# A retention layer's prompt states, computed from split keys and values as single-rate matrix products

## The chip, the cores and the metric

The kernel runs on one core of a Trainium2 chip. The metric is the device time of one execution in microseconds (us); lower is better. A core has five engines with queues of their own: TensorE (PE, matrix products; its weight loads are listed as PEld), VectorE (DVE), ScalarE (ACT), GpSimd (POOL) and SyncE (SP), which here issues the DMA transfers. SBUF is the memory on the core, PSUM the memory that TensorE writes its products to.

## The reference, cut to what matters

One layer of a hybrid decoder: a feed-forward half step, a mixer, another feed-forward half step, each with a layer norm. The mixer runs a retention branch (8 heads, keys and values 256 wide) beside an HGRN2 branch (16 heads of 128). It handles 16 meta tokens and 256 prompt tokens, and 8 sample sequences of one token each. For each retention head the prompt leaves a state, the sum over the prompt's tokens of key (outer) value, each key scaled by the head's decay up to the last token:

```
def retention_chunk(S, q, k, v):
    ...
    k_dec = k * jnp.exp(lg[:, None] * (C - 1.0 - idx))[:, :, None].astype(k.dtype)
    S_new = jnp.exp(lg * C)[:, None, None].astype(S.dtype) * S + jnp.einsum('bhjd,bhjv->bhdv', k_dec, v)
    return S_new.astype(S.dtype), o
```

These states (`state_ret_prompt`, 8 heads of 256 x 256) are one of the six outputs. All numbers are float32.

## The kernel before

Activations lie with features on the partitions and the 280 tokens (272 prompt, 8 samples) along the free axis. Every large weight is read in units of eight 128x128 blocks (512 KB): SyncE loads a unit into `raw` (three buffers), ScalarE rounds it to the single-rate type float32r (`whi`, line 145), and VectorE takes the difference (`wlo`, line 147). Activations are split in the same way. A dense product is then three single-rate products per block: high x high, high x low, low x high (lines 169 to 171). `whi` and `wlo` have three buffers each.

The order of TensorE's instructions is that in which the program emits them. The other engines' and SyncE's orders are laid out by a scheduler at build time, in which the weight units have high priority; each engine then executes its queue in order, and each instruction waits for its operands.

In the mixer the input projection is the dense stream, head by head: for head u the groups f, q_h, i_h, q_r, k_r, v_r, then the gates of head u - 1. Beside it run two "threads", Python generators: `mix_hg` (HGRN2) and `mix_ret` (retention). After each k step of the dense stream (in a group of two outputs that is six products), `pump` counts down each thread's wait; when it is zero, the thread emits its next piece. `yield 12` thus means that the thread's next piece stands 12 steps later in TensorE's order.

`mix_ret` for one head, with the names used below:

- For each half c of the 256 features: values are transposed on TensorE in three blocks of tokens (128, 128, and the last 24: 16 prompt tokens and 8 samples) into a PSUM bank `pt` and copied by ScalarE into `vtr` and `vt2` (lines 711, 712). Keys are transposed likewise, and VectorE multiplies them by the decay `dec` into `ktr` and `kt2` (line 718). The decay of the 8 samples' rows is zero. PSUM banks of the tag `mx` go round in four, for both threads.
- Scores: products of keys and queries (`psc`), multiplied by the table `dtab`.
- States: for each half, three full-precision products of keys and values into `psr` (line 743), copied to `sro` and written out (lines 746, 747).
- Samples, in two parts e of four samples: `vbr` holds the sample's value on all partitions (read back by a DMA). For each half, `smr` (three buffers of 512 KB) receives four samples' states by DMA (line 761), ScalarE scales it by the decay (line 762), VectorE adds key times value (line 765), and it is written out (line 768). After `yield 12` TensorE multiplies it with the queries (`pqr`, line 774).
- Outputs of the prompt (`por`), norm (`pvr`) and the rest.

In `mix_hg`, the product `po` of line 681 reads `osh`, which ScalarE copies in line 674 from `pq`.

Of the kernel before, what the change touches and what calls it, by code (L numbers as in the profile page):

```python
# [10 lines left out]
F32 = mybir.dt.float32  # L11
F32R = mybir.dt.float32r
U8 = mybir.dt.uint8
AF = mybir.ActivationFunctionType
ALU = mybir.AluOpType
# [3 lines left out]
P = 128  # L19
# [78 lines left out]
def trunk(ctx: ExitStack, tc: tile.TileContext, A, O):  # L98
    nc = tc.nc
# [12 lines left out]
    def mx_bank(name):  # L112
        return ps_m.tile([P, 512], F32, tag="mx", name=name)
# [12 lines left out]
    dec = cst.tile([P, 3, HR], F32, tag="dec", name="dec")  # L126
# [48 lines left out]
    def split(hi, lo, x):  # L175
        nc.scalar.copy(hi, x)  # L176
        nc.vector.tensor_tensor(out=lo, in0=x, in1=hi.bitcast(F32), op=ALU.subtract)  # L177
# [6 lines left out]
    def mul(out, a, b):  # L184
        nc.vector.tensor_tensor(out=out, in0=a, in1=b, op=ALU.mult)
# [4 lines left out]
    def sub(out, a, b):  # L190
        nc.vector.tensor_tensor(out=out, in0=a, in1=b, op=ALU.subtract)  # L191
# [195 lines left out]
    with tc.tile_pool(name="yp", bufs=1) as yp:  # L387
        yh, yl = [None] * KC, [None] * KC
        with tc.tile_pool(name="mp", bufs=1) as mp:
# [7 lines left out]
            def tmp(name, shape=(P, T), bufs=1, dt=F32, tag=None):  # L397
                if name in rows:
                    rows[name] = rows[name][1:] + rows[name][:1]
                    return rp.tile(list(shape), dt, tag=rows[name][-1], name=name)  # L400
                return mp.tile(list(shape), dt, tag=tag or name, name=name, bufs=bufs)
# [24 lines left out]

            km = tmp("km", (P, P))
            vm = tmp("vm", (P, 2, 2, P))
            kt2 = tmp("kt2", (P, 2, P))
            vt2 = tmp("vt2", (P, 2, P))  # L430
            scr2 = tmp("scr2", (P, NMETA))
            for z in (km, vm, kt2, vt2, scr2):
                nc.gpsimd.memset(z, 0.0)
            threads = []

            def pump(_=None):
# [87 lines left out]
            BLOCKS = ((0, P), (P, P), (2 * P, T - 2 * P))  # L524

            def rows_out(src, width, tag):

                scr = drp.tile([NS, width], F32, tag=tag + "d", name=tag + "d")
                nc.sync.dma_start(scr, src)
                return scr  # L530
# [170 lines left out]

            def mix_ret(u, q, k, v):
                vt = tmp("vtr", (P, 2, 2, P))
                kt = tmp("ktr", (P, 2, 2, P))
                dt = tmp("dtab", (P, NSC))
                nc.sync.dma_start(dt, A["dtab"][u])
                for c in range(2):
                    pt = mx_bank("pt")
                    for b, (t0, n) in enumerate(BLOCKS):
                        nc.tensor.transpose(pt[:n, b * P : (b + 1) * P], v[:, c, t0 : t0 + n], ident)  # L710
                    nc.scalar.copy(vt[:, :, c, :], pt[:, : 2 * P].rearrange("p (b f) -> p b f", b=2))
                    nc.scalar.copy(vt2[: BLOCKS[2][1], c, :], pt[: BLOCKS[2][1], 2 * P : 3 * P])
                    yield 1
                    pt = mx_bank("pt")
                    for b, (t0, n) in enumerate(BLOCKS):
                        nc.tensor.transpose(pt[:n, b * P : (b + 1) * P], k[:, c, t0 : t0 + n], ident)
                    for b, (t0, n) in enumerate(BLOCKS):
                        nc.vector.tensor_scalar(
                            out=(kt[:, b, c, :] if b < 2 else kt2[:n, c, :]), in0=pt[:n, b * P : (b + 1) * P],
                            scalar1=dec[:n, b, u : u + 1], scalar2=None, op0=ALU.mult)  # L720
                    yield 2
                nc.vector.tensor_copy(qdr[:, :, 0 : NS * 32 : 33], q[:, :, SEQ:])
                vts = [vt[:, 0], vt[:, 1], vt2]
                kts = [kt[:, 0], kt[:, 1], kt2]
                vrow = rows_out(vt2.rearrange("p c f -> p (c f)")[16:24, :], 256, "vr")

                psc = mx_bank("psc")
                for b, (col, l0, n, nk) in enumerate(SCORES):
                    for c in range(2):
                        nc.tensor.matmul(  # L730
                            psc[:nk, col : col + n], k[:, c, b * P : b * P + nk], q[:, c, l0 : l0 + n],
                            start=c == 0, stop=c == 1)
                scr = dt
                c2 = SCORES[2][0]
                mul(scr[:, :c2], psc[:, :c2], dt[:, :c2])
                mul(scr2[:NB2], psc[:NB2, c2:NSC], dt[:NB2, c2:])
                scrs = [scr[:, SCORES[0][0] : SCORES[1][0]], scr[:, SCORES[1][0] : c2], scr2]
                yield 2

                for c in range(2):  # L740
                    pst = mx_bank("psr")
                    for b in range(3):
                        nc.tensor.matmul(
                            pst[:, :256], kts[b][:, c, :], vts[b].rearrange("p c f -> p (c f)"), start=b == 0, stop=b == 2)
                    so = tmp("sro", (P, 256))
                    nc.scalar.copy(so, pst[:, :256])
                    nc.sync.dma_start(O["srp"][u, c], so)
                    yield 2

                centre(vt.rearrange("p b c f -> p b (c f)"))  # L750
                centre(vt2.rearrange("p c f -> p (c f)").unsqueeze(1))

                os = tmp("osr", (P, 256))
                for e in range(2):
                    vb = tmp("vbr", (P, 4, 256))
                    nc.sync.dma_start(vb, vrow[4 * e : 4 * e + 4, :].partition_broadcast(P))
                    sms = []
                    for c in range(2):
                        sm = tmp("smr", (P, 4, 256), bufs=3)
                        sms.append(sm)  # L760
                        nc.sync.dma_start(sm, A["sr"][u, c, :, 4 * e : 4 * e + 4, :])
                        nc.scalar.mul(sm, sm, GAMMA[u])
                        for j in range(4):
                            t = LP + 4 * e + j
                            nc.vector.scalar_tensor_tensor(  # L765
                                out=sm[:, j, :], in0=vb[:, j, :], scalar=k[:, c, t : t + 1], in1=sm[:, j, :],
                                op0=ALU.mult, op1=ALU.add)
                        nc.sync.dma_start(O["srs"][u, c, :, 4 * e : 4 * e + 4, :], sm)
                    yield 12
                    pq = mx_bank("pqr")  # L770
                    for c in range(2):
                        for j in range(4):
                            b = 4 * e + j
                            nc.tensor.matmul(
                                pq[32 * j : 32 * j + 32, :256], qdr[:, c, 32 * b : 32 * b + 32], sms[c][:, j, :],
                                start=c == 0, stop=c == 1, tile_position=(0, 32 * j))
                    if e == 0:
                        nc.scalar.copy(os, pq[:, :256])
                    else:
                        add(os, os, pq[:, :256])  # L780
                centre(os.unsqueeze(1))
                yield 7

                on = tmp("on_r", (P, 2, TL), bufs=2)
                on_r[u] = on
                for c in range(2):
                    po = mx_bank("por")
                    for b, (col, l0, n, nk) in enumerate(SCORES):
                        nc.tensor.matmul(po[:, l0 : l0 + n], vts[b][:, c, :], scrs[b], start=b == 0, stop=b == 2)
                    nc.tensor.matmul(po[:, SEQ:TL], os[:, c * P : (c + 1) * P], sel, start=True, stop=True)  # L790
                    nc.scalar.copy(on[:, c, :], po[:, :TL])
                    yield 1
                sqs = tmp("sqr", (P, TL)), tmp("sq2", (P, TL))
                for c in range(2):
                    nc.scalar.activation(sqs[c], on[:, c, :], AF.Square)
                add(sqs[0], sqs[0], sqs[1])
                hilo = tmp("rhi", (P, TL), dt=F32R), tmp("rlo", (P, TL), dt=F32R)
                split(*hilo, sqs[0])
                yield 7
                pv = mx_bank("pvr")  # L800
                sums(pv[:, :TL], hilo)
                r = rsqrt(lambda name: tmp(name, (P, TL)), pv[:, :TL], 1.0 / 256, eps_h)
                for c in range(2):
                    mul(on[:, c, :], on[:, c, :], r)
                done_r.add(u)
# [131 lines left out]
```

## Time and profile before

| | |
|---|---|
| median of 3 runs | 2847.35 us (2843.78 to 2848.24) |
| the profiled execution | 2841.64 us |
| its span, first to last instruction | 2839.6 us |
| granted TensorE clock | 0.997 |
| busy share: TensorE, VectorE, ScalarE | 98%, 60%, 46% |
| HBM traffic | 188 GB/s over the span |

Rows of the profile name a source line of the kernel, the engine, the operation, output<-inputs by the program's names, the tile (partitions x elements) and the count. In a list of groups follow the busy time in us and the mean ns of one instruction, then the engine's idle time before them and what ended it. In a list in order of time the first number is the start in us, the second the length of the merged rows, and a bracket gives the idle time before and its releaser. Names that differ only in digits are merged, so `vt2` is shown as vt, `kt2` as kt, and the three groups of `pt` banks as pt. Products overlap in TensorE's pipeline, so the distance between two starts tells what a product costs in a stream, not the length of its row. "SPq" is SyncE's queue of DMA issues.

### The profile page before, as it was taken

The numbers are of one execution on the slowest core, as the hardware profiler recorded it, in microseconds if no ns is written. First come the engines' busy times: TensorE is split into PE (matmuls) and PEld (weight loads), VectorE is DVE, ScalarE is ACT, GpSimd is POOL, SyncE is SP. The second block draws the span as 40 slices with busy tenths as digits, with TensorE's granted clock in tenths as the row PEclk, the third lists the DMA queues.
The fourth block names the chain that finished last, engine by engine and source line by source line (L and its number), as shares of the span: only waits on it lengthen the run. The fifth ranks groups of instructions, "written<-read, shape, count | busy, mean of one in ns | idle before, by whom it ended". The sixth has DMA issues, their size and how long they took to land. (4 is left out here: it accounts for less than half of the span.)

```text
span 2839.6 us, 54221 instructions
## 1 busy us (share of the span) xinstructions
PE 2796.7 (98%) x22626; PEld 2760.7 (97%) x22626; DVE 1712.0 (60%) x2754; ACT 1317.9 (46%) x1921; POOL 4.5 (0%) x43
## 2 busy tenths in 40 slices
PE   8999999999999999999999999999999999999997
PEld 8999999999999999999999999999999999999997
DVE  5444444455578767666766676765884444445555
ACT  4443444433354564545454555545554444444333
POOL 0000000000000000000000000000000000000000
PEclk9999999999999999999999999999999999999998
DMA  6455555445555665756565657565555555555553
GB/s 214 171 171 171 170 170 171 170 168 171 170 193 189 221 241 178 244 177 241 178 240 184 239 180 245 179 217 171 179 178 182 180 184 180 183 180 180 181 182 128
DMA packets 155718, 536.26 MB, mean 189 GB/s; under 512 B 18064, under 2 KB 27856, under 8 KB 155472
## 3 DMA queue, kind: packets, MB, share of 16 engines
q1 hardware_dynamic: 155472, 532.80, 55.4%
q8 instruction: 177, 2.90, 0.4%
q14 instruction: 69, 0.57, 0.1%
HBM read 502.12 MB, written 30.61 MB: 188 GB/s over the span
## 5 line engine op out<-in xcount | busy, mean ns | idle before, releaser
L147 DVE TENSOR_TENSOR wlo<-raw,whi 128x1024 fp32r<-128x1024 f32 x868 | 1063.1, 1225 | 899.4 <-ACT whi L145 895.6
L145 ACT CAST whi<-raw 128x1024 fp32r<-128x1024 f32 x868 | 909.0, 1047 | 1160.3 <-PE up L170 481.8
L169 PE MATMUL up<-xh,whi 128*128 128x280 f32 (+1 forms) x2688 | 773.2, 288 | 8.6 <-ACT xh L176 8.6
L170 PE MATMUL up<-xl,whi 128*128 128x280 f32 (+1 forms) x2688 | 774.5, 288 | 1.3 <-DVE xl L177 1.2
L171 PE MATMUL up<-xh,wlo 128*128 128x280 f32 (+1 forms) x2688 | 773.6, 288 | 0.0
L169 PEld LDWEIGHTS up<-xh,whi 128*128 128x128 f32 x2688 | 506.8, 189 | 8.6 <-ACT xh L176 8.6
L170 PEld LDWEIGHTS up<-xl,whi 128*128 128x128 f32 x2688 | 506.5, 188 | 2.1 <-DVE xl L177 2.1
L171 PEld LDWEIGHTS up<-xh,wlo 128*128 128x128 f32 x2688 | 506.8, 189 | 0.0
L169 PE MATMUL dn<-hh,whi 128*128 128x280 f32 (+1 forms) x1376 | 397.1, 289 | 0.0
L170 PE MATMUL dn<-hl,whi 128*128 128x280 f32 (+1 forms) x1376 | 395.8, 288 | 0.0
L171 PE MATMUL dn<-hh,wlo 128*128 128x280 f32 (+1 forms) x1376 | 395.7, 288 | 0.0
L170 PEld LDWEIGHTS dn<-hl,whi 128*128 128x128 f32 x1376 | 259.0, 188 | 0.1
L169 PEld LDWEIGHTS dn<-hh,whi 128*128 128x128 f32 x1376 | 258.9, 188 | 0.1
L171 PEld LDWEIGHTS dn<-hh,wlo 128*128 128x128 f32 x1376 | 258.6, 188 | 0.0
L765 DVE SCALAR_TENSOR_TENSOR smr<-vbr,k_r,smr 128x256 f32<-128x256 f32 x128 | 54.1, 480 | 55.2 <-DMA vbr<-vrd 33.6
L169 PE MATMUL pj_g_r<-xh,whi 128*128 128x264 f32 x256 | 82.9, 324 | 0.0
L170 PE MATMUL pj_i_h<-xl,whi 128*128 128x280 f32 x256 | 74.9, 293 | 2.6 <-DVE xl L324 2.6
L169 PE MATMUL pj_v_r<-xh,whi 128*128 128x280 f32 x256 | 76.6, 299 | 0.0
L169 PE MATMUL pj_i_h<-xh,whi 128*128 128x280 f32 x256 | 75.0, 293 | 0.7 <-ACT xh L323 0.7
L169 PE MATMUL pj_k_r<-xh,whi 128*128 128x280 f32 x256 | 75.2, 294 | 0.0
L171 PE MATMUL pj_v_r<-xh,wlo 128*128 128x280 f32 x256 | 74.6, 291 | 0.0
L170 PE MATMUL pj_v_r<-xl,whi 128*128 128x280 f32 x256 | 74.6, 291 | 0.0
(324 smaller groups left out, 5178.0 us busy)
## 6 DMA issues: line engine op xcount, KB each, us to landing
raw<-in_w_up SPq DMA_DIRECT2D x344, 512.0 KB, 3.5
raw<-in_w_in SPq DMA_DIRECT2D x320, 512.0 KB, 3.6
raw<-in_w_dn SPq DMA_DIRECT2D x172, 512.0 KB, 3.4
smr<-in_sr SPq DMA_DIRECT2D x32, 512.0 KB, 7.1
out_srs<-smr SPq DMA_DIRECT2D x32, 512.0 KB, 3.4
raw<-in_w_out SPq DMA_DIRECT2D x32, 512.0 KB, 3.4
smh<-in_sg SPq DMA_DIRECT2D x16, 512.0 KB, 4.3
out_sgs<-smh SPq DMA_DIRECT2D x16, 512.0 KB, 4.3
```

Of the source, the lines that this page charges most:

```text
L145: nc.scalar.copy(hi, raw)
L147: nc.vector.tensor_tensor(out=lo, in0=raw, in1=hi.bitcast(F32), op=ALU.subtract)
L169: nc.tensor.matmul(o, wh, h, start=k == 0, stop=False)
L170: nc.tensor.matmul(o, wh, l, start=False, stop=False)
L171: nc.tensor.matmul(o, wl, h, start=False, stop=k == nk - 1)
L765: nc.vector.scalar_tensor_tensor(out=sm[:, j, :], in0=vb[:, j, :], scalar=k[:, c, t : t + 1], in1=sm[:, j, :], op0=ALU.mult, op1=ALU.add)
```

## The change

For the retention states alone, keys and values are split into a high part (rounded to float32r) and a low part (the difference). For each of the two full token blocks and each half there are three single-rate products (high x high, high x low, low x high). The last block has only 24 rows, so its three products are stacked in one: the key tile `ks2` holds high, high, low at rows 0, 32 and 64, and the value tile `vs2` holds high, low, high; the rest of both is zero. A half's state is then seven single-rate products in place of three full-precision ones. The high parts of the keys come from ScalarE (`activation` with the decay as scale), the low parts from VectorE. The split tiles `ks` and `vs` use two of the three buffers of the tag `smr`, and the wait ahead of the sample products is 14 steps in place of 12. `vtr` and `vt2` stay, as the prompt's outputs still read them; `ktr` and `kt2` go.

```
-            kt2 = tmp("kt2", (P, 2, P))
...
+            ks2 = tmp("ks2", (P, 2, P), dt=F32R)
+            vs2 = tmp("vs2", (P, 2, P), dt=F32R)
+            for z in (km, vm, vt2, scr2):
                 nc.gpsimd.memset(z, 0.0)
+            for z in (ks2, vs2):
+                nc.scalar.copy(z.rearrange("p c f -> p (c f)"), vm.rearrange("p h b f -> p (h b f)")[:, : 2 * P])
...
             def mix_ret(u, q, k, v):
                 vt = tmp("vtr", (P, 2, 2, P))
-                kt = tmp("ktr", (P, 2, 2, P))
+                ks, vs = (tmp(n, (P, 2, 2, 2 * P), dt=F32R, bufs=3, tag="smr") for n in ("ks", "vs"))
+                NB = BLOCKS[2][1]
+                third = [slice(32 * i, 32 * i + NB) for i in range(3)]
...
                     nc.scalar.copy(vt[:, :, c, :], pt[:, : 2 * P].rearrange("p (b f) -> p b f", b=2))
-                    nc.scalar.copy(vt2[: BLOCKS[2][1], c, :], pt[: BLOCKS[2][1], 2 * P : 3 * P])
+                    nc.scalar.copy(vt2[:NB, c, :], pt[:NB, 2 * P : 3 * P])
+                    f = slice(c * P, (c + 1) * P)
+                    split(vs[:, 0, :, f], vs[:, 1, :, f], vt[:, :, c, :])
+                    nc.scalar.copy(vs2[third[0], c, :], vt2[:NB, c, :])
+                    nc.scalar.copy(vs2[third[2], c, :], vt2[:NB, c, :])
+                    sub(vs2[third[1], c, :], vt2[:NB, c, :], vs2[third[0], c, :].bitcast(F32))
                     yield 1
...
                     for b, (t0, n) in enumerate(BLOCKS):
-                        nc.vector.tensor_scalar(
-                            out=(kt[:, b, c, :] if b < 2 else kt2[:n, c, :]), in0=pt[:n, b * P : (b + 1) * P],
-                            scalar1=dec[:n, b, u : u + 1], scalar2=None, op0=ALU.mult)
+                        x, g = pt[:n, b * P : (b + 1) * P], dec[:n, b, u : u + 1]
+                        his = [ks[:, 0, b, f]] if b < 2 else [ks2[third[0], c, :], ks2[third[1], c, :]]
+                        for hi in his:
+                            nc.scalar.activation(hi, x, AF.Copy, scale=g)
+                        nc.vector.scalar_tensor_tensor(
+                            out=(ks[:, 1, b, f] if b < 2 else ks2[third[2], c, :]), in0=x, scalar=g,
+                            in1=his[0].bitcast(F32), op0=ALU.mult, op1=ALU.subtract)
...
                 for c in range(2):
                     pst = mx_bank("psr")
-                    for b in range(3):
-                        nc.tensor.matmul(
-                            pst[:, :256], kts[b][:, c, :], vts[b].rearrange("p c f -> p (c f)"), start=b == 0, stop=b == 2)
+                    f = slice(c * P, (c + 1) * P)
+                    pairs = [(ks[:, i, b, f], vs[:, j, b, :]) for b in range(2) for i, j in ((0, 0), (0, 1), (1, 0))]
+                    pairs.append((ks2[:, c, :], vs2.rearrange("p c f -> p (c f)")))
+                    for i, (kk, vv) in enumerate(pairs):
+                        nc.tensor.matmul(pst[:, :256], kk, vv, start=i == 0, stop=i == 6)
...
-                    yield 12
+                    yield 14
```

More of the change, by code (lines that the diff above doesn't have):

```diff
@@ L428, in trunk @@
             vm = tmp("vm", (P, 2, 2, P))
-            kt2 = tmp("kt2", (P, 2, P))
             vt2 = tmp("vt2", (P, 2, P))
             scr2 = tmp("scr2", (P, NMETA))
-            for z in (km, vm, kt2, vt2, scr2):
+            ks2 = tmp("ks2", (P, 2, P), dt=F32R)
+            vs2 = tmp("vs2", (P, 2, P), dt=F32R)
+            for z in (km, vm, vt2, scr2):
                 nc.gpsimd.memset(z, 0.0)
+            for z in (ks2, vs2):
+                nc.scalar.copy(z.rearrange("p c f -> p (c f)"), vm.rearrange("p h b f -> p (h b f)")[:, : 2 * P])
             threads = []
@@ L723, in mix_ret @@
                 vts = [vt[:, 0], vt[:, 1], vt2]
-                kts = [kt[:, 0], kt[:, 1], kt2]
                 vrow = rows_out(vt2.rearrange("p c f -> p (c f)")[16:24, :], 256, "vr")
```

## The prediction

> **What bounds the kernel now.** I read the page's busy shares first, then the waits of TensorE, then the busy time in the mixer's stretch, then TensorE in order of time around one head's state products.
>
> ```profile
> span 2839.6 us, 54221 instructions
> ...
> PE 2796.7 (98%) x22626; PEld 2760.7 (97%) x22626; DVE 1712.0 (60%) x2754; ACT 1317.9 (46%) x1921; POOL 4.5 (0%) x43
> ```
>
> ```profile
> PE up L169 <- ACT xh L176: 8.6, 1, 8.6
> ...
> PE po L681 <- ACT osh L674: 3.6, 5, 0.8
> ```
>
> ```profile
> 890.00:1920.00 1030.00, 1021.58 (x8475) 990.24 (x8474) 716.26 (x1373) 549.57 (x936) 0.79 (x8) 1.00 0.62 211
> ```
>
> TensorE is busy for 98% of the span. The two rows of its waits are the longest at the kernel's start (8.6 us, once) and the longest inside the mixer (3.6 us over five heads). The third row is the stretch in which the eight heads' prompt states are made: its columns are length, then busy time (and count) of TensorE, its weight loads, VectorE, ScalarE and GpSimd, then clock, DMA share and GB/s. TensorE has 1021.6 of 1030 us, VectorE 716 (70%), ScalarE 550 (53%). So a microsecond of TensorE's work taken out of the mixer is a microsecond off the end, as long as no product has to wait for a new operand. The question is the size of the saving, and whether the new splits and the moved loads make TensorE wait.
>
> **Part 1: the products.** Head 7, first half, in TensorE's order of time:
>
> ```profile
> 1870.70 1.03 PE L743 MATMUL psr<-vtr,ktr 128*128 128x256 f32 x4
> 1871.56 0.59 PE L743 MATMUL psr<-vt,kt 128*128 128x256 f32 x2
> ...
> 1872.11 0.28 PE L170 MATMUL pj_g_r<-xl,whi 128*128 128x264 f32 x1
> ```
>
> ```profile
> L743 PEld LDWEIGHTS psr<-vtr,ktr x64: 187/188/191, 911.0 to 1873.9; 128*128 128x128 f32 x64
> L743 PE MATMUL psr<-vtr,ktr x64: 377/378/380, 911.1 to 1874.1; 128*128 128x256 f32 x64
> ...
> L743 PE MATMUL psr<-vt,kt x32: 379/379/379, 912.0 to 1874.5; 128*128 128x256 f32 x32
> ```
>
> ```profile
> 964.88 0.28 PE L182 MATMUL pl<-prodsmh,ones_r 128*128 128x256 f32 x1
> 965.00 0.28 PE L182 MATMUL pl<-prodvbh,ones_r 128*128 128x256 f32 x1
> 965.12 0.28 PE L169 MATMUL pj_q_r<-xh,whi 128*128 128x264 f32 x1
> ```
>
> The program has three full-precision products in each of 16 groups (eight heads, two halves), and the records are 64 + 32 = 96: each is issued as two. From the first of the six records (1870.70) to the second dense product behind them (1872.11) are 1.41 us; with one dense product of 0.12 us between, a group takes 1.29 us, 0.215 us a record. The price of the new products stands in the third fence: line 182 already multiplies single-rate operands, 256 columns wide, with a weight load each, one record a product, and the starts are 0.12 us apart. Seven of them are 0.84 us. The saving is 1.29 - 0.84 = 0.45 us a group, and 16 x 0.45 = 7.2 us. The starts are rounded to 0.01 us; if the true spacing is 0.115, a group costs 0.805 and the saving is 7.8; at 0.125 it is 6.6. I take 7.2.
>
> The Trainium skill, "TensorE: Matmul & The Clock Gate", section "Back-to-back issue gap", gives N/2.4 + 2.5 ns between warm products, an estimate of 109 ns at 256 columns: seven would be 0.76 us and the saving 8.5 us. The row of 0.12 us decides against it here; I keep 8.5 only as a sign of which side an error would lie on.
>
> **Part 2: the splits on ScalarE and VectorE.** Prices by shape:
>
> ```profile
> L648 ACT ACTIVATE smh<-smh,fk 128x128 f32<-128x128 f32 x128 | 41.8, 392 | 9.5 <-DMA smh<-in_sg 8.1 <-DVE wlo L147 1.3
> ...
> L176 ACT CAST prodsmh<-pr 128x256 fp32r<-128x256 f32 x40 | 14.8, 405 | 8.3 <-PE pl L182 6.7 <-DVE pr L185 1.6
> ...
> L660 ACT COPY Sh<-pst 128x128 f32<-128x128 f32 x16 | 4.1, 259 | 0.0
> ...
> L712 ACT COPY vt<-pt 24x128 f32<-24x128 f32 x16 | 4.0, 251 | 0.0
> ```
>
> ```profile
> L177 DVE TENSOR_TENSOR prodvbh<-pr,prodsmh 128x256 fp32r<-128x256 f32 x40 | 15.5, 420 | 0.0
> ...
> L662 DVE SCALAR_TENSOR_TENSOR Sh<-Sh,T,pst 128x128 f32<-128x128 f32 x32 | 11.1, 346 | 0.5
> ...
> L718 DVE TENSOR_SCALAR ktr<-pt,dec 128x128 f32<-128x128 f32 x32 | 9.7, 345 | 2.1 <-PE pt L716 2.1
> ...
> L718 DVE TENSOR_SCALAR kt<-pt,dec 24x128 f32<-24x128 f32 x16 | 5.3, 329 | 0.0
> ```
>
> ScalarE gains seven instructions a half: one cast of 128x256 values (0.405), two 24-row copies of values (2 x 0.251), two scaled key parts of 128x128 (0.259 as a copy from PSUM, 0.392 as a scaled one; no row has both, I take 0.33), two of 24 rows (2 x 0.25). That is 2.07 us a half and 4.1 us a head, 3.8 to 4.4 by the two ends. VectorE gains the value's low part (0.420) and its 24 rows (0.33, nearest L718); the three key operations change form at the same price (346 against 345 ns). That is 0.75 us a half, 1.5 us a head. Neither engine is the bound: ScalarE goes from 53% to 57%, VectorE from 70% to 71%. What counts is the stretch before the first state product:
>
> ```profile
> 1861.20:1870.70 9.50, 9.50 (x81) 8.93 (x81) 6.12 (x14) 3.92 (x9) 0.00 (x0) 1.00 0.50 163
> ```
>
> ```profile
> 1864.84 0.38 ACT L711 COPY vtr<-pt 128x256 f32<-128x256 f32 x1 [1.65 <-PE pt L710]
> ```
>
> In the 9.5 us from the first values in PSUM to the state products ScalarE is busy for 3.9 and VectorE for 6.1; with 4.1 and 1.5 more they reach 8.0 and 7.6. Both fit, though in order. The last values reach ScalarE at 1864.84; behind it stand 0.6 us of copies, 0.9 us of value parts, 1.1 us of keys and a weight cast (1.05, which may come first): the operands are there by about 1868.5, 2 us ahead of 1870.70. The key bank in PSUM is read for longer (four ScalarE operations and three of VectorE, not three), and four such banks go round; it is free by about 1866, and the score products that take the fourth bank start behind that. I cost this part at nothing; its cover is these 2 us, and 0 to 1 us a head is its bound, 0 to 8 us in all. Zeroing two tiles once on ScalarE replaces one memset on GpSimd; two copies (0.8 us at L176's price) before the mixer's products at worst.
>
> **Part 3: the moved state loads.** The split tiles take two of the three "smr" buffers, in which the samples' states are loaded. Before, three loads can be issued ahead of the head. Now one can; the second and third must wait until the second half's products have read the split tiles. The yield of 14 for 12 puts each of the two sample products two steps later; a step is six dense products, 0.73 us, so 1.46 us. Head 7, TensorE, SyncE, ScalarE and VectorE in turn:
>
> ```profile
> 1873.45 1.02 PE L743 MATMUL psr<-vtr,ktr 128*128 128x256 f32 x4
> ...
> 1885.72 1.07 PE L774 MATMUL pqr<-smr,qdr 128*32 128x256 f32 x16
> ...
> 1896.64 0.39 PE L681 MATMUL po<-sel,osh 128*128 128x8 f32 x2 [0.70 <-ACT osh L674]
> ```
>
> ```profile
> 1876.09 0.38 SPq L143 DMA_DIRECT2D raw<-in_w_in  x1
> ...
> 1889.05 0.42 SPq L761 DMA_DIRECT2D smr<-in_sr  x1
> ```
>
> ```profile
> 1895.10 1.06 ACT L762 ACTIVATE smr<-smr 128x1024 f32<-128x1024 f32 x1 [3.47 <-DMA smr<-in_sr]
> ...
> 1896.33 0.26 ACT L674 COPY osh<-pq 128x128 f32<-128x128 f32 x1
> ```
>
> ```profile
> 1885.17 1.67 DVE L765 SCALAR_TENSOR_TENSOR smr<-vbr,k_r,smr 128x256 f32<-128x256 f32 x4 [2.94 <-DMA vbr<-vrd]
> ...
> 1896.19 1.68 DVE L765 SCALAR_TENSOR_TENSOR smr<-vbr,k_r,smr 128x256 f32<-128x256 f32 x4 [3.30 <-ACT smr L762]
> ```
>
> After the change, on this clock: the second half starts at 1873.0 and ends at about 1874.0. The load can then be issued, lands 6.05 us later (1889.05 to 1895.10), is scaled (1.06) and updated (1.67): about 1883 to 1884. The product that needs it stands at 1885.72 - 0.9 (two groups shorter) + 1.46 = 1886.3. Slack 2 to 3 us, so nothing on TensorE's path. The late end: SyncE is held behind the weight load of 1876.09, ScalarE behind a weight cast (1.05), VectorE behind its own (1.2 us): 1876.5 + 6.05 + 1.05 + 1.06 + 1.2 + 1.67 = 1887.5, 1.2 us late. Behind the waiting load in SyncE's queue stand weight loads, behind the waiting scale ScalarE's weight casts; they run two buffers (about 16 dense blocks, 6 us) ahead of TensorE, and today's waits of 3.47 and 2.94 us in these queues cost TensorE nothing. The second sample product has its operand at 1897.87 now and starts at 1898.52, 0.65 us; two more yields move it 1.46 us away from its load, so that slack grows.
>
> **Sum.** 2841.64 us (this execution; its span and 2.04 us around it) - 7.2 = 2834.4. The three runs have a median of 2847.35, 5.7 above this execution; on that scale it is 2840.1. About 0.2% (5.7 us) is what a measurement can tell from no change.
>
> **Rivals.**
> *The other thread's wait grows (no change).* The wait at 1896.64 is the other mixer's product, whose operand is copied at 1896.33, in ScalarE's order behind the scale that waited 3.47 us for its load. If that load moves the 1.46 us of the new yield against the other thread and the order stays, five heads wait 1.46 us longer: 7.3 us, all of the saving, 2847.4. Against it: at 1889.05 the load was issued behind a weight load and an output, not straight behind the product of 1885.72. If instead the copy goes first, the 3.6 us of today's waits fall away: 2836.5.
> *The state load comes late (slower).* Part 3's late end, 1.2 us in each of eight heads, is 9.6 us, 2.4 us slower than before: 2849.7. The point from which it decides is 0.9 us a head; beyond 1.6 us a head the kernel is slower by over 0.2%, say 2 us: 2856. For it: loads and products come close, and ScalarE and VectorE are in order. Against: it takes three queues late together in every head.
> *Operands of the first half late.* Part 2's cover gone: up to 1 us a head, 2848.
> *Weight loads do not hide.* Were each of seven products spaced by its load (0.188), a group would take 1.32 us, 0.03 more than now, and the time would be 2847.8. The stream of full-array loads at 0.12 us a product speaks against it. The Trainium skill, same page, Part 3, "The mechanism", says that a load overlaps products in flight only when the row group differs, a rule that by itself asks for this case; the trace does not agree.
>
> **How the numbers follow.** My sum within about 1.5 us: 0.50. The saving with today's waits gone too: 0.07. Part of it eaten, or all of it, by the other thread or late operands: 0.29. Late state loads: 0.13. Unhidden weight loads: 0.01. Above 5.7 us of gain lie most of the first and all of the second, with little of the third: 0.53 faster. Slower by over 0.2% takes 1.6 us a head: 0.10. The rest, 0.37, is the same. The range goes from today's waits gone (2836.5) less 3.5, as the runs reach 3.57 below their median, to the late loads (2849.7): 2833 to 2850. The likeliest case alone is 2837 to 2842.
>
> **What would show it.** Right: 112 single-rate records for the state products, starts 0.12 us apart, and no TensorE wait on "ks", "vs", "smr" or the keys' bank. Wrong: TensorE waits before the state products on ScalarE or VectorE, before the sample product on "smr", or longer waits on "osh"; or a group of seven over 0.9 us.

## The result, and the profile after

The changed kernel takes 2827.36 us (median of 6 runs, 2825.25 to 2830.10) against 2845.88 us for the kernel before (6 runs, 2843.78 to 2848.24): a ratio of 0.9937 [0.9928, 0.9947], 18.5 us faster. The profiled execution took 2827.42 us. The forecast was 2840.1 us and a range of 2833 to 2850, so the sign was right and the gain more than twice the one forecast, outside the range.

The changed kernel, first the span and the busy shares of its page, then waits of TensorE (us in all, times, longest):

```profile
span 2825.5 us, 54397 instructions
PE 2789.3 (99%) x22642; PEld 2758.0 (98%) x22642; DVE 1725.2 (61%) x2786; ACT 1354.2 (48%) x2035; POOL 4.3 (0%) x42
```

```profile
PE up L169 <- ACT xh L176: 8.8, 2, 8.6
PE pd L182 <- ACT prodsmh L176: 2.7, 2, 2.0
...
PE pst L662 <- ACT km L646: 1.4, 1, 1.4
```

TensorE works 7.4 us less (2796.7 to 2789.3), and the span is 14.1 us shorter. So about half of the gain is work taken out and half is idle time taken out. The rows of `po` behind `osh` (3.6 us before) and of `pvr` behind `rlo` are gone. The second is a row of the kernel before that the prediction did not show:

```profile
PE pvr L182 <- DVE rlo L177: 2.6, 7, 0.5
...
PE pst L657 <- ACT km L641: 0.7, 1, 0.7
```

Two stretches in the middle of the mixer, the kernel before and then the one after (length, busy time and count of TensorE, its loads, VectorE, ScalarE, GpSimd, clock, DMA share, GB/s):

```profile
1200.00:1500.00 300.00, 297.91 (x2474) 289.50 (x2474) 207.38 (x391) 159.74 (x268) 0.00 (x0) 1.00 0.62 208
1500.00:1800.00 300.00, 298.50 (x2471) 290.62 (x2470) 207.23 (x391) 161.53 (x267) 0.00 (x0) 1.00 0.61 207
```

```profile
1200.00:1500.00 300.00, 300.00 (x2516) 293.01 (x2516) 213.32 (x402) 173.21 (x301) 0.00 (x0) 1.00 0.61 210
1500.00:1800.00 300.00, 300.00 (x2508) 293.38 (x2507) 217.60 (x419) 171.29 (x299) 0.00 (x0) 1.00 0.62 210
```

In these 600 us TensorE idled for 3.6 us before and does not idle at all after.

For a finer account I took TensorE's records in order of time between the first dense product of the projection and the first of `wo` (called the mixer below), and summed by how much each distance between two starts exceeds the middle value for the same pair of shapes, where it does so by more than 0.06 us. The mixer is 1159.9 us before and 1145.7 us after, 14.2 us apart. Of these 7.4 are the state products: from the first product of a group to the second dense product behind it are 1.42 us before and 0.95 after, 0.46 us in each of 16 groups. Ahead of `po` stood 4.4 us of excess before and none after; ahead of `pvr` 3.8 and none; ahead of `pst` 1.0 and 1.6; ahead of `pd` and `pl`, early products of the HGRN2 thread, 4.2 and 5.3. 7.4 + 4.4 + 3.8 - 0.6 - 1.1 is 13.9 of the 14.2. (An excess is larger than the wait that the profile lists: 4.4 against 3.6, 3.8 against 2.6.)

Where the wait of `pvr` went is seen in head 7, TensorE in order of time and below it VectorE's making of `rlo`, before and then after:

```profile
1907.94 0.37 PE L790 MATMUL por<-sel,osr 128*128 128x8 f32 x2
...
1914.08 0.29 PE L182 MATMUL pvr<-rhi,ones_r 128*128 128x264 f32 x1
...
1914.84 0.39 PE L182 MATMUL pvr<-rlo,ones_r 128*128 128x264 f32 x1 [0.47 <-DVE rlo L177]
...
1914.36 0.43 DVE L177 TENSOR_TENSOR rlo<-sqr,rhi 128x264 fp32r<-128x264 f32 x1
```

```profile
1897.48 0.37 PE L808 MATMUL por<-sel,osr 128*128 128x8 f32 x2
...
1902.89 0.38 PE L662 MATMUL pst<-vm,km 128*128 128x128 f32 x2
1903.11 0.39 PE L663 MATMUL pst<-vth,kth 128*128 128x128 f32 x2
1903.33 0.39 PE L664 MATMUL pst<-vth,kth 128*128 128x128 f32 x2
...
1904.28 0.28 PE L182 MATMUL pvr<-rhi,ones_r 128*128 128x264 f32 x1
1904.40 0.29 PE L182 MATMUL pvr<-rlo,ones_r 128*128 128x264 f32 x1
...
1903.73 0.42 DVE L177 TENSOR_TENSOR rlo<-sqr,rhi 128x264 fp32r<-128x264 f32 x1
```

Between the last `por` and `pvr` ScalarE and VectorE must copy `por`, square, sum and split it. Before, only 48 dense products stand between (6.14 us), and `rlo` comes late. After, six records of the other thread's `pst` stand there too, 6.80 us in all, and nothing waits. The chain itself is nearly as long: from the last `por` to the end of `rlo` are 6.85 us before and 6.67 after. So it is the distance on TensorE that took the wait away, with about 0.25 us to spare (`rlo` is read at 6.92). The same products stand between in heads 1 to 7 of each kernel; head 0 has others in both.

The wait of `po` went on ScalarE (after, head 7):

```profile
1879.36 1.06 ACT L780 ACTIVATE smr<-smr 128x1024 f32<-128x1024 f32 x1
1880.30 0.27 ACT L679 COPY osh<-pq 128x128 f32<-128x128 f32 x1
...
1882.73 1.05 ACT L780 ACTIVATE smr<-smr 128x1024 f32<-128x1024 f32 x1
```

Before, `osh` was copied behind a scale of `smr` that had waited 3.47 us for its load. Now it is copied ahead of the last scale, and the scale ahead of it has not waited. Between `pq` and `po` TensorE still has the same 18 dense products (2.87 us).

### The profile page after: what moved, and what is told of

Read it like the earlier page. It is cut to its first block, busy times and chain, and to the rows that moved or that the text cites. A ratio compares the mean times of both kernels' runs of the same rounds, so it can differ in the third digit from the quotient of the medians.

```text
span 2825.5 us, 54397 instructions
## 1 busy us (share of the span) xinstructions
PE 2789.3 (99%) x22642; PEld 2758.0 (98%) x22642; DVE 1725.2 (61%) x2786; ACT 1354.2 (48%) x2035; POOL 4.3 (0%) x42
## 4 chain that ended last, share of the span: by engine, by line
PE 97%; DVE 1%; DMA 1%; ACT 0%; issue 0%; SPq 0%; ACTq 0%; DVEq 0%
PE up L170 12%; PE up L171 12%; PE up L169 12%; PE dn L169 6%; PE dn L170 6%; PE dn L171 6%; PE pj_g_r L169 1%; PE pj_v_r L169 1%; PE pj_f L169 1%; PE pj_g_h L169 1%; PE pj_k_r L169 1%; PE pj_f L170 1%; PE pj_k_r L170 1%; PE pj_v_r L170 1%; PE pj_f L171 1%; PE pj_v_r L171 1%
## 5 line engine op out<-in xcount | busy, mean ns | idle before, releaser
L169 PE MATMUL pj_g_h<-xh,whi 128*128 128x264 f32 x256 | 75.7, 296 | 0.0
L171 PE MATMUL pj_i_h<-xh,wlo 128*128 128x280 f32 x256 | 75.2, 294 | 0.0
```

The lines of the kernel that those rows point to most:

```text
L169: nc.tensor.matmul(o, wh, h, start=k == 0, stop=False)
L171: nc.tensor.matmul(o, wl, h, start=False, stop=k == nk - 1)
```

## The experiments

Theory A at the start: the products give 7.2 us, and the rest is the waits that disappeared, partly because the profiled execution of before had fewer of them than its other runs. Theory B: the products give the whole gain, the new form costing less than 0.84 us a group. Theory C: the moved loads, or the yield, give the rest by themselves.

**The kernel before again**, unchanged.

> The kernel before, once more. In the profiled execution of before TensorE's waits inside the mixer add up to 13.7 us, in that of after to 7.0, and the seven products save 7.4 us by TensorE's starts (0.93 us a head): together the 14.1 us between the two spans. The medians differ by 18.5. Theory A (the waits of before vary from run to run, and its profiled execution had few of them): this profile shows more than 13.7 us of waits, 16 to 19, on osh, rlo or smr. Theory B (the products are worth more in the ordinary runs): the waits are again 13 to 14 us and the groups of products dearer than 1.29 us. Ratio to before 1.000 in both.

Measured: 2843.76 us, ratio 0.9999 [0.9990, 1.0008]. Its profiled execution has a mixer of 1164.1 us, 4.2 longer than the one used for the forecast. The difference is one wait in head 0, that of `pst` for `km` (waits of TensorE):

```profile
PE pst L657 <- ACT km L641: 4.8, 1, 4.8
PE po L681 <- ACT osh L674: 3.2, 4, 1.6
PE pvr L182 <- DVE rlo L177: 2.8, 7, 0.5
```

`km` waited there on ScalarE behind scales whose loads came late:

```profile
929.46 1.87 ACT L648 ACTIVATE smh<-smh,fk 128x128 f32<-128x128 f32 x6 [2.38 <-DMA smh<-in_sg]
...
937.87 1.06 ACT L762 ACTIVATE smr<-smr 128x1024 f32<-128x1024 f32 x1 [3.53 <-DMA smr<-in_sr]
...
942.13 0.25 ACT L641 COPY km<-ptk 16x128 f32<-16x128 f32 x1
```

So two executions of the kernel before differ by about 4 us of luck in one wait. That would account for most of the 4.4 us between the spans' 14.1 us and the medians' 18.5; the waits of the unprofiled runs are not known. **The kernel after again** in the same way:

> The changed kernel once more, to stand beside the other three on the same chip: 0.993 to 0.995 of before, 2826 to 2829, mixer length 1145 to 1147 us.

Measured: 2828.73 us, 0.9944 [0.9931, 0.9956], mixer 1148.2 us, its `km` wait 2.7 us where it was 1.4. By the two ratios the gain is 16 and 18 us (by the medians 15.4 and 18.5).

**The new products taken out again**, splits, loads and yield kept. The low parts of the two full blocks are computed but not used, so the states have the precision of the high parts there.

```
-  pairs = [(ks[:, i, b, f], vs[:, j, b, :]) for b in range(2) for i, j in ((0, 0), (0, 1), (1, 0))]
+  pairs = [(ks[:, 0, b, f].bitcast(F32), vs[:, 0, b, :].bitcast(F32)) for b in range(2)]
   ... (ks2, vs2) bitcast likewise, stop=i == 2
```

> The changed kernel, its splits, buffers and yield, but with three full-precision products of the high parts in each group in place of the seven single-rate ones (the low parts are left out of the product). It undoes the cheaper products alone. The sum of the prediction, corrected by the trace: 16 x 0.465 = 7.4 us slower than after, 2834 to 2836, with after's waits. If the products are worth all 18.5 us: 2845.

Measured: 2835.80 us, 0.9967 [0.9954, 0.9979]; mixer 1152.9 us. Full-precision products cost 7.2 us more in the mixer (1152.9 - 1145.7) and 8.4 us in the medians. (In this execution the `km` wait is missing and one sample product takes 1.3 us longer, which nearly cancel; by the starts of its own groups the term is 7.5 us.) That is the forecast's term, and it leaves about 9 us of gain in a kernel that has no cheaper product. Theory B falls.

**Each group's seven products twice**, the second pass over the first.

```
+  for r in range(2):
       for i, (kk, vv) in enumerate(pairs):
```

> The changed kernel with each group's seven products made twice (the second time over the first). 112 products more at 0.12 us: 13.4 us more than after, 2839.5 to 2842, with no new waits. At 0.109 us a product it would be 12.2; if weight loads do not hide (0.188), 21.

Measured: 2839.39 us, 0.9979 [0.9970, 0.9989]; 12.0 us over the kernel after, 11.8 us in the mixer. The `km` wait of 1.4 us is missing in this execution, so 13.2 us belong to 112 products, 0.118 us each; the starts of the groups themselves give the same 13.2. The products stand 0.12 us apart in the kernel after, with loads of 188 ns (rows of one tile: shortest, middle, longest in ns, first and last start):

```profile
L762 PEld LDWEIGHTS psr<-vs,ks x112: 187/188/193, 910.9 to 1862.1; 128*128 128x128 f32 x112
L762 PE MATMUL psr<-vs,ks x112: 274/282/287, 911.1 to 1862.2; 128*128 128x256 f32 x112
```

**The yield of 14 alone**, in the kernel before.

```
-  yield 12
+  yield 14
```

> The kernel before with the yield of 14 in place of 12 and nothing else. Theory Y (the later sample products take the waits away): TensorE's waits on osh and rlo go, 6 us or more, 2835 to 2840 us against 2846. Theory L (the moved state loads take them away): no change, 2844 to 2848. Theory P (all of the gain comes from the products): no change.

Measured: 2840.84 us, 0.9988 [0.9979, 0.9997]; mixer 1159.9. `pvr` no longer waits, as `pst` stands ahead of it in heads 1 to 7. But `po` waits longer, and in head 7 ScalarE shows why (the waits of TensorE, then ScalarE in order of time):

```profile
PE po L681 <- ACT osh L674: 4.6, 4, 1.8
```

```profile
1896.28 1.06 ACT L762 ACTIVATE smr<-smr 128x1024 f32<-128x1024 f32 x1 [4.57 <-DMA smr<-in_sr]
...
1897.51 0.26 ACT L674 COPY osh<-pq 128x128 f32<-128x128 f32 x1
```

The load's wait grew from 3.47 to 4.57 us with `osh` still behind it. This is the mechanism of the prediction's first rival, and it is what the yield does by itself; its size is 1.0 us in all (3.6 to 4.6), where the rival had 7.3.

**The kernel after with the yield of 12.**

```
-  yield 14
+  yield 12
```

> The changed kernel with the old yield of 12. Theory Y: the waits come back, only the products' 7.4 us stay, 2837 to 2840. Theory L: nothing comes back, 2826 to 2831. If the state load is late for the sample product (the rival of the prediction), waits on smr appear and it is slower still, above 2840.

Measured: 2854.90 us, 1.0037 [1.0024, 1.0049]; slower than before by about 10 us, with a mixer of 1173.8 us. I had not expected a loss of that size. Waits of TensorE:

```profile
PE pvr L182 <- DVE rlo L177: 6.3, 7, 0.9
PE pvr L182 <- ACT rhi L176: 4.5, 7, 0.6
PE pst L662 <- ACT km L646: 2.5, 1, 2.5
...
PE pqr L792 <- DVE smr L783: 1.6, 4, 0.7
```

`pvr` stands behind 48 dense products alone again and now waits twice, for `rhi` and for `rlo`, in heads 1 to 7: 13.8 us of excess in the mixer.

The row of `pqr` is small, but its cost is not. Head 7, the last load of the samples' states, its scale, its update and the second sample product; below them the same product in the kernel after:

```profile
1902.90 0.43 SPq L779 DMA_DIRECT2D smr<-in_sr  x1
...
1909.04 1.06 ACT L780 ACTIVATE smr<-smr 128x1024 f32<-128x1024 f32 x1 [0.97 <-DMA smr<-in_sr]
...
1910.14 1.67 DVE L783 SCALAR_TENSOR_TENSOR smr<-vbr,k_r,smr 128x256 f32<-128x256 f32 x4
...
1910.12 2.36 PE L792 MATMUL pqr<-smr,qdr 128*32 128x256 f32 x16
```

```profile
1888.04 1.07 PE L792 MATMUL pqr<-smr,qdr 128*32 128x256 f32 x16
```

The last eight of the product's sixteen records go here at the pace of VectorE's four updates, two records about every 0.40 us, where the kernel after has them 0.007 us apart in groups of four. Hardly any idle time is listed between them, as each record is 0.38 us long and the next start comes before its end. In heads 1 to 7 the second sample product is 0.5 to 2.1 us longer than in the kernel after, 9.4 us in all. This is the prediction's second rival, the late state load. It happens with the yield of 12; in both profiles of the kernel after, with 14, no sample product is stretched.

**The moved loads alone.** Two `smr` buffers are held from the head's start until the second half's state has been copied, as `ks` and `vs` hold them, with no split and the products of before; once with the yield of 12 and once with 14. Holding them takes four one-column copies a head on ScalarE.

```
+  holds = [tmp(n, (P, 2, 2, 2 * P), bufs=3, tag="smr") for n in ("hk", "hv")]
+  for hd in holds: nc.scalar.copy(hd[:, 0, 0, :1], eps_h)
   ...                       # behind the second half's copy of psr
+  for hd in holds: nc.scalar.copy(hd[:, 0, 0, :1], pst[:, :1])
```

> The kernel before, with two of the three smr buffers held from the head's start until the second half's state product is copied, as the split tiles hold them after the change: only the samples' state loads move (and four copies of one column a head hold the buffers). Yield 12, no splits, full-precision products. The table so far, in the mixer's length from its first product to the first of w_out: before 1159.9 and 1164.1, yield 14 alone 1159.9, the changed kernel with yield 12 1173.8, with yield 14 and full products 1152.9. Theory L (moved loads take the osh waits away but bring the sample products and the norm's products too close at 12): osh waits go, pvr waits grow to about 10 us, time 2850 to 2862. Theory S (the splits on ScalarE make the pvr waits): pvr waits stay at 2.6 to 2.8, time 2838 to 2846.

> The same with yield 14: the two moves together, no split and no cheaper product. Theory of two parts: the waits on osh and rlo all go, as in the changed kernel, and the time is that of the changed kernel with full products, 2834 to 2838, so that over half of the gain has nothing to do with the products. If the splits play a part in it: 2840 to 2846.

Measured at 12: 2852.99 us, 1.0028 [1.0018, 1.0039], mixer 1166.8. At 14: 2835.64 us, 0.9967 [0.9955, 0.9979], mixer 1152.9. The waits of TensorE at 12, and two stretches of the mixer at 12 and at 14:

```profile
PE pvr L182 <- ACT rhi L176: 6.1, 6, 1.2
PE po L681 <- ACT osh L674: 2.8, 6, 0.7
```

```profile
1200.00:1500.00 300.00, 296.85 (x2450) 288.19 (x2450) 207.05 (x391) 161.51 (x274) 0.00 (x0) 1.00 0.61 207
1500.00:1800.00 300.00, 296.87 (x2460) 288.06 (x2460) 204.56 (x383) 159.48 (x273) 0.00 (x0) 1.00 0.61 207
```

```profile
1200.00:1500.00 300.00, 300.00 (x2492) 291.90 (x2492) 209.08 (x392) 163.59 (x280) 0.00 (x0) 1.00 0.61 208
1500.00:1800.00 300.00, 300.00 (x2490) 292.75 (x2489) 211.15 (x399) 164.16 (x277) 0.00 (x0) 1.00 0.62 210
```

Neither edit gives the rest alone: the yield gives 3.7 us in the medians, the moved loads lose 8.5 (each against the run of before beside it). Together they give 8.9 us and leave TensorE without idle time in these stretches. So theory C falls: it is the pair. And 2835.64 us is the 2835.80 us of the kernel that also makes all the splits, so at a yield of 14 the splits cost nothing that these runs can tell. At 12 they do: 1173.8 us against 1166.8 us, although the products are 7.2 us cheaper, so about 14 us between these two executions. 8.4 of these are the stretched sample products (9.4 against 1.1), 4.0 are excess ahead of `pvr` (13.8 against 9.8) and 2.7 ahead of `pst`, while `po` waits less. The size is not firm: the moved loads at 12 ran from 2847.18 to 2859.82 us, the profiled execution (2848.98) was among the faster ones, and by the medians the splits cost about 9 us there.

**Yields of 13 and 16** in the kernel after.

> The changed kernel with a yield of 13. The norm's chain falls 2 x 0.73 = 1.46 us earlier than at 14 beside the other thread. If the waits fade in steps with the slack: between 12 (2854.9) and 14 (2827.4), 2832 to 2845. If 13 is already clear of ScalarE's table load and scales: 2827 to 2830.

> The changed kernel with a yield of 16. After's own heads 2 to 7 show no wait at 14. Theory of placement (what counts is where the retention thread's chain on ScalarE falls beside the other thread's work, and 14 happens to fall clear): 16 can be as good, 2825 to 2830, or bring other waits back. If later is simply better: below 2827, as head 0's wait on km (1.36 in after's profile) would go too.

Measured: 13 gives 2843.22 us, 0.9996 [0.9987, 1.0005]; 16 gives 2830.48 us, 0.9951 [0.9938, 0.9965], beside 2828.73 us for 14 on the same chip. At 13 `pst` is not yet ahead of `pvr`, and the waits are those of 12 (head 7):

```profile
1909.73 0.37 PE L808 MATMUL por<-sel,osr 128*128 128x8 f32 x2
...
1916.63 0.39 PE L182 MATMUL pvr<-rhi,ones_r 128*128 128x264 f32 x1 [0.59 <-ACT rhi L176]
...
1917.93 0.39 PE L182 MATMUL pvr<-rlo,ones_r 128*128 128x264 f32 x1 [0.91 <-DVE rlo L177]
```

At 16 `pst` still is, but the other side loses its cover. Between the second `pqr` and `por` the kernel after has five records of `pv` and `ptk` beside 42 dense products (6.77 us in head 7); at 16 these two have gone ahead, 6.22 us are left, and a new row appears, in heads 2 to 7:

```profile
PE por L808 <- DVE osr L705: 4.5, 6, 1.1
```

The profiled execution was the slowest of the five (2836.47 us), so the row need not be as large in the others, and the medians do not tell 16 from 14.

**More steps for the first heads' HGRN2 thread**, against the `km` wait. In the first of two kernels, three waits of that thread are longer; head 1's thread then writes its sample queries (at 937.55 us) before head 0's last sample product (959.29), which reads those in place of its own, so the samples' output is wrong and only the time is of use.

```
e9   yield 9 if u > 1 else (12 if u else 9)     # was: 9 if u else 5
     yield 14 if u else 10                      # was: 14 if u else 6
e12  yield 9 if u > 1 else (11 if u else 7)     # was: 9 if u else 5
```

> The changed kernel, with HGRN2's thread given more steps where after still waits: the first wait 9 for 5 in head 0 and 12 for 9 in head 1, and the two waits ahead of head 0's states 10 for 6. Waits of after that it aims at: 1.97 and 0.68 on prodsmh, 1.16 on prodvbh, 1.36 on km, together 5.2 us. Expected 2822 to 2825; unchanged if the waits only move.

> The changed kernel with two steps more for HGRN2's thread ahead of its first product in heads 0 and 1 (7 for 5, 11 for 9). It aims at the waits on prodsmh and prodvbh of after (1.97, 0.68, 1.16). Two steps are 1.46 us: expected 2823 to 2826, 2 to 4 us below after in the same call. Unchanged if the waits go elsewhere.

Measured: 2828.80 us, 0.9941 [0.9928, 0.9953], and 2826.64 us, 0.9937 [0.9925, 0.9950]. The second has a shorter `km` wait than the kernel after beside it (1.6 against 2.7 us) but new ones behind `osh` (0.9 us) and `rlo` (0.8 us); the first has 2.9 us behind `osh` and 1.2 us behind `rhi`. The intervals overlap with that of the kernel after: no version here is shown to be better than it.

## Why the prediction was wrong

The step that failed is part 3, which entered the yield and the moved loads as nothing. The forecast of 2840.1 us lies 12.7 us above the result: 7.0 us are for the most part waits that went away (2834.4 forecast and 2827.4 measured for the profiled execution), and 5.7 us are the distance to the median that was carried over.

- *Part 1, the products.* Right: 7.2 us forecast, 7.4 us measured by the groups' own starts and 7.2 by taking the products out again. The record spacing of 0.215 and 0.12 us in the trace of before carried the whole term. The Trainium skill, "TensorE: Matmul & The Clock Gate", section "Back-to-back issue gap", gives the formula behind the 109 ns for an isolated product; the 8.5 us by it are not what the mixer shows, and doubled products cost 0.118 us each. The medians' 8.4 us do not separate the two.
- *Part 2, the splits.* Nothing, as costed, with the yield of 14. TensorE has no wait on `ks` or `vs`, but the cover was not the 2 us named. In head 7 the operands of the first half were complete 2.6 us ahead of its product (1856.61 and 1859.17), those of the second half 1.1 us ahead of its own (1860.38 and 1861.47), after the first half's product had begun. The cover that mattered was another, the one ahead of `pvr`, as the yield of 12 shows. ScalarE's busy time in the stretch from 890 to 1920 us rose by 46 us (549.57 to 595.99) where 33 were forecast. The seven instructions take 2.43 us a half by their lengths where 2.07 were forecast (a scaled key part is 0.36 us in both shapes), 39 us in all; the stretch also holds more work, as the kernel runs ahead.
- *Part 3, the yield and the moved loads.* This is the step that failed. That the sample products do not wait for `smr` was right, but the whole part was then entered in the sum as zero. It was worth 8.2 us in the profiled pair, 4.4 at `po` and 3.8 at `pvr`, of which 1.7 came back ahead of `pst`, `pd` and `pl`. Two things were missed. The 2.6 us row of `pvr` was not priced at all, since nothing of the change touches `pvr`; but the yield moves the retention thread's whole tail against the other thread, and so decides what stands between `por` and `pvr`. And a yield was counted in steps of dense products alone, 0.73 us each, where its effect is a jump, when a product of the other thread changes sides.
- *The first rival and its reverse.* The mechanism was named, the chances were set the wrong way round. "The other thread's wait grows" happened with the yield alone; with the moved loads beside it the copy went first, which the prediction priced at 3.6 us and gave 0.07. Its 2836.5 us less the `pvr` row would have been 2833.9, still 6.5 us above the result.
- *The sum.* 5.7 us between the profiled execution and the median were carried over as they stood. They are no property of both kernels: after the change the profiled execution is at the median (2827.42 and 2827.36 us). The two profiled executions of before differ by one wait, `km` in head 0 (0.7 and 4.8 us), and the forecast's was the one without it; in those of after it is 1.4 and 2.7 us.
- *The other rivals.* Late operands did not happen at 14, and late state loads did not either; with the yield of 12 the late state loads cost 9.4 us, so the two steps that the yield adds are what keeps them off. Weight loads hid: 112 full-array loads of 0.188 us at 0.12 us a product, against the rule of the Trainium skill's same page, Part 3, "The mechanism", that a load overlaps products in flight only when the row group differs.

What stays open: why ScalarE's and VectorE's order puts the chain ahead of `pvr` later with moved loads alone, since the order is the scheduler's; and, for the same reason, why the last state loads come late at 12 with the splits and hardly without them.

## What to carry to other kernels

Where two instruction streams are interleaved on one engine, price a change of one wait by listing what stands between each product and its consumer in both streams, before and after, and not by the steps it moves. Every listed wait in that stretch is a term of the sum, also those that the change does not touch. Before a spare microsecond is called cover, ask whose operand it covers.

## What the runs showed that I had not expected

How narrow the placement is: with one number changed in the kernel after, 12, 13, 14 and 16 give 2854.9, 2843.2, 2828.7 and 2830.5 us, a spread (26 us) larger than the products' saving. The runs at 14 and 16 are not told apart. And a wait costs TensorE more than the idle time listed with it: at the yield of 12 the 10.8 us of `pvr` waits are 13.8 us of excess between starts, and the 1.6 us of `pqr` waits are 9.4.
